# Issue order of the high and low weight products in the routed experts of a two-layer decoder trunk

## Chip, cores and metric

The kernel runs on one core of a Trainium2 chip. The metric is the time of one execution in microseconds (us) on the device; lower is better. A core has a tensor engine (PE, with its weight loads shown as PEld), VectorE (DVE), ScalarE (ACT), GpSimd (POOL) and SyncE (SP), and 16 DMA engines that move data between DRAM and the on-chip memory.

## What is computed

512 tokens of 1,024 features pass through two layers. Layer 0 is a gated short convolution and a dense SwiGLU; layer 1 is latent attention with 8 heads and then a mixture of 8 experts, of which each token uses two. The change touches the experts alone:

```python
def swiglu(h, w_gate, w_up, w_down):
    return (jax.nn.silu(h @ w_gate) * (h @ w_up)) @ w_down

def moe_swiglu(h, router, w_gate, w_up, w_down):
    ...
    probs = jax.nn.softmax((ht @ router).astype(jnp.float32), axis=-1)
    vals, idx = lax.top_k(probs, TOP_K)
    wts = vals / jnp.sum(vals, axis=-1, keepdims=True)
    gates = jnp.einsum('tk,tke->te', wts, jax.nn.one_hot(idx, N_EXPERTS, dtype=jnp.float32)).astype(h.dtype)
    out = jnp.zeros_like(ht)
    for e in range(N_EXPERTS):
        out = out + gates[:, e:e + 1] * swiglu(ht, w_gate[e], w_up[e], w_down[e])
    return out.reshape(bsz, seq, d)
```

An expert's `w_gate` and `w_up` are 1024 x 2048, its `w_down` 2048 x 1024, all float32.

## The kernel before

To keep float32 accuracy, every weight chunk is split on the chip into a high part (`w_hi`, type fp32r, by a ScalarE copy at line 88) and a low part (`w_lo`, what is left over, bf16 in the experts, by a VectorE subtraction at line 97). The activations are split likewise: `xe` and `ae` hold a high and a low part side by side, `xb` and `ab` a bf16 copy. The high weights meet both parts of the activations in one product that is 2 x cap columns wide; the low weights meet the bf16 copy in one product of cap columns. Both add into the same PSUM tile `gu`. "cap" is the number of token rows that an expert handles without a branch: 152 for the first three experts, then 148, 140, 132, 128 and 128.

One weight chunk is 128 x 2048, that is 16 weight blocks of 128 x 128 and 1 MB in DRAM. An expert has 24 chunks, c = 0 to 23; the 8 experts have 192. Chunks 0 to 15 give the hidden features: each holds 8 blocks of the gate and 8 of the up projection (`hidden_mm`). Chunks 16 to 23 are the down projection, 16 blocks to one column of the output (`down_mm`). Both call `row`, which before the change has three nested loops: over the part (high, then low), over the PSUM columns, over the blocks. So a chunk is 16 high products (line 1030) followed by 16 low ones (line 1032). The first down chunk is issued in two pieces, 14 blocks and then the last 2 (`late`), because the last hidden features come late.

The order of all engines' work in this part is written out by hand: `manual_schedule`, and a loop over the experts and their 24 chunks. In step c of that loop stand, in this order,

- the products of chunk c;
- the gate of a hidden chunk: a ScalarE copy and a VectorE addition (lines 1044, 1045) that fold the two halves of `gu`, a Silu on ScalarE (line 1050), the product with the up half on GpSimd (line 1051), and one and two steps later its split (lines 1055 to 1057);
- the high split of chunk c+3 and the low split of chunk c+2;
- the load of a chunk to come, from the SP queue (line 75).

The split parts have three buffers each. Each engine works strictly in the order written. Besides, steps 1 to 4 of an expert transpose and store the rows of the expert before it: two transfers from GpSimd's queue that add into DRAM (line 1083), one of each half of the rows, in steps 2 and 4. Step 3 selects and step 6 finds and gathers the tokens of the next expert, also with GpSimd's transfers (line 993), and steps 16 to 22 transpose what was gathered. A loop for tokens beyond an expert's cap follows at the end; it uses the same `row`.

Of the kernel before, what the change touches and what calls it, by code (L numbers as in the profile page):

```python
# [28 lines left out]
NE = 8  # L29
# rows of an expert that are computed without a branch: of the first two, then of the others from the one with most  # L30
# tokens to the one with fewest; what an expert has beyond them is left to a loop
CAPS = (152, 152, 152, 148, 140, 132, 128, 128)
# [20 lines left out]
class Stream:  # L53
# [8 lines left out]
    def grow(self, pool, n):  # L62
        """n more places for chunks to come, the next to be used."""
        self.ring = [(pool, n)] * n + self.ring
# [91 lines left out]
def hybrid_trunk_kernel(ctx, tc, xT_in, pos_in, vecs_in, rope_g, invf_in, ident_in, cst_in, info_in, dslot_in,  # L156
# [31 lines left out]

    # the first 24 weight blocks come with the features that they meet
    vec = cpool.tile([P, NV], F32, name="vec")  # L190
# [109 lines left out]

# [1 line left out]
    with tc.tile_pool(name="dn", bufs=1) as dn, tc.tile_pool(name="dt", bufs=2) as dt, \  # L302
# [99 lines left out]

# [1 line left out]
    man = ExitStack()  # L404
# [25 lines left out]
    def split_next(n=4):  # L430
        """The next weight chunk's two parts, in n steps; then the load of a chunk to come."""
        k = ws.n_split
        w = ws.chunks[k][1]
        ws.hi[k], ws.lo[k] = [ws.pool.tile([P, CW], F32R, name=t, tag=t, bufs=2) for t in ("w_hi", "w_lo")]
        ws.n_split += 1
        ws.n_lo += 1

        def step(i):
            c = slice(i * w // n, (i + 1) * w // n)
            hi, raw = ws.hi[k][:, c], ws.raw[k][:, c]  # L440
            nc.scalar.copy(hi, raw)  # L441

            def low():
                tt(ws.lo[k][:, c], raw, hi.bitcast(F32), ALU.subtract)
                if i == n - 1:
                    del ws.raw[k]
                    if ws.n_raw < ws.raw_limit:
                        list(ws.load())
            return [low]
        return [partial(step, i) for i in range(n)]  # L450
# [3 lines left out]
    def emit(*items):  # L454
        """One slot: the items' products now, what reads them in the slots after it, a stage in each."""
        now = []
        for f in items:
            for n, stage in enumerate(f() or ()):
                now.append((slot[0] + 1 + n, stage))
        ready = [x for x in due if x[0] <= slot[0]]  # L460
        due[:] = [x for x in due if x[0] > slot[0]] + now
        for _, stage in sorted(ready, key=lambda x: x[0]):
            stage()
        slot[0] += 1
# [308 lines left out]

    # the slots of a pair's attention: scores and probabilities of both heads, the first head's values, weight splits
    lay = [dict(n=15, S=(0, 1, 2, 3, 7, 8, 9, 10), T=(4, 5, 6, 7, 11, 12, 13, 14), V=11, W=(6, 9, 11, 13)),
# [7 lines left out]
    def plan(hp):  # L783
        """A pair's attention, slot by slot, with the next pair's operands and the last pair's output rows among it."""
        cur, nxt, prv, y = pairs[hp], pairs[hp + 1] if hp < 3 else None, pairs[hp - 1] if hp else None, lay[hp]
# [62 lines left out]

# [1 line left out]
    acc = xpool.tile([P, T], F32, name="acc")  # L850
# [48 lines left out]
    bp = bctx.enter_context(tc.tile_pool(name="bp", bufs=6, side="right", reuse_waits="tile"))  # L899
    # token rows, normalised, in two parts: tr[part][half of the features]  # L900
    tr = [[None, quarter(part, 1)] for part in "hl"]
# [15 lines left out]
    def base(i, copy):  # L917
        """The sum so far of a token row: what the experts' rows are added to."""
        hf, tb = divmod(i, TB)
        hs = bp.tile([P, T], F32, name="hs")  # L920
        copy(hs, hps[i])
        nc.sync.dma_start(out[tb * P:(tb + 1) * P, hf * T:(hf + 1) * T], hs)
# [23 lines left out]
    def keep_warm(n):  # L946
        """Products that nothing reads, so that the tensor engine's clock isn't lowered while it waits."""
        for _ in range(n):
            mm(idle, ones_b, ones_b[:, None, :].to_broadcast([P, TB, P]), start=True, stop=True)
# [6 lines left out]

# [1 line left out]
    class Expert:  # L958
# [61 lines left out]
        def row(s, ps, hl, n, x2, xb, flip, late=()):  # L1020
            """ps[i] += one column block of 128; hl[i]: its n weight blocks (hi, lo)."""
            order = [k for k in range(n) if k not in late]
            for kcs in (order, list(late)):
                for part in ((1, 0) if flip else (0, 1)):
                    for i, p in enumerate(ps):
                        for kc in kcs:
                            first = kc == order[0] and part == (1 if flip else 0)
                            final = kc == (late or order)[-1] and part == (0 if flip else 1)
                            if part == 0:
                                mm(p[:, 0:2 * s.cap], hl[i][kc][0], x2[:, kc, :, :], start=first, stop=final)  # L1030
                            else:
                                mm(p[:, 0:s.cap], hl[i][kc][1], xb[:, kc, :], start=first, stop=final)  # L1032

# [57 lines left out]

# [1 line left out]
    ws.grow(ctx.enter_context(tc.tile_pool(name="mraw2", bufs=1, reuse_waits="tile")), 1)  # L1093
# [25 lines left out]
    b = lg[:, :, :, None].to_broadcast(sh4)  # L1119
    # a stands before b in the ranks where a - b is at least this: a tie goes to the lower index  # L1120
    least = least.rearrange("p (a b) -> p a b", a=NE)
# [5 lines left out]
    ts(sel_b, rank, 2.0, None, op0=ALU.is_lt)  # L1127
    # pos: an expert's tokens counted from 1, 0 where it isn't chosen
    mm(pc, tri, sel, start=True, stop=False)
# [11 lines left out]

    # the first two experts' tokens, by one-hot products
    c2 = CAPS[0]
# [76 lines left out]
    def rank_experts():  # L1220
        """perm[r, e]: expert e of those beyond NS has the RANKS[r]-th most tokens of them."""
        a = cnt[:, None, NS:].to_broadcast([P, NO, NO])
        b = cnt[:, NS:, None].to_broadcast([P, NO, NO])
        eq = tmp([NO, NO], "eq")
        tt(eq, a, b, ALU.subtract)
        tt(eq, eq, least[:, NS:, NS:], ALU.is_ge)
        at = tmp([NO], "at")
        nc.vector.tensor_reduce(at, eq, axis=AX.X, op=ALU.add)
        tt(perm, at[:, None, :].to_broadcast([P, NO, NO]), place[:, :, None].to_broadcast([P, NO, NO]), ALU.is_equal)
        tt(eq, perm, iota[:, None, NS - 1:NE - 1].to_broadcast([P, NO, NO]), ALU.mult)  # L1230
        nc.vector.tensor_reduce(at, eq, axis=AX.X, op=ALU.add)
        nc.vector.tensor_copy(ids, at)
# [12 lines left out]
    def ranked_weights():  # L1245
        """The weights of an expert known by its rank: where they lie comes from the table of indices."""
        for r in range(NO):
            e = nc.values_load(ids[0:1, r:r + 1], engines=[mybir.EngineType.SP], min_val=NS, max_val=NE - 1)
            for c in range(24):
                k = n_dense + (NS + r) * 24 + c  # L1250
                ws.chunks[k] = (w_moe[ds(e * 24 + c, 1)].rearrange("o p w -> (o p) w"), 2048, BF16)
# [5 lines left out]
    def extra_rows():  # L1257
        """How many blocks of CAP rows each expert has beyond its capacity, and whether there are any."""
        t = tmp([NO, NO], "eq")
        tt(t, perm.rearrange("p r e -> p e r"), short[:, None, NS:].to_broadcast([P, NO, NO]), ALU.mult)  # L1260
        nc.vector.tensor_copy(adj[:, 0:NS], short[:, 0:NS])
        nc.vector.tensor_reduce(adj[:, NS:], t, axis=AX.X, op=ALU.add)
        nx, n = tmp([NE + 1], "nx"), tmp([NE], "n")
        tt(cnt, cnt, adj, ALU.add)
        ts(nx[:, 0:NE], cnt, float(CAP), None, op0=ALU.is_gt)
        for i in (2, 3):
            ts(n, cnt, float(i * CAP), None, op0=ALU.is_gt)
            tt(nx[:, 0:NE], nx[:, 0:NE], n, ALU.add)
        nc.vector.tensor_reduce(nx[:, NE:], nx[:, 0:NE], axis=AX.X, op=ALU.max)
        nc.vector.tensor_copy(extra, nx)  # L1270
# [66 lines left out]

# [1 line left out]
    tab = dram.tile([NE * ROWS, 16], I32, name="tab")  # L1339
# [100 lines left out]

# [1 line left out]
def _host(inp):  # L1442
# [94 lines left out]
```

## Time and profile before

| what | value |
|---|---|
| median of 3 runs | 1513.46 us (1513.43 to 1515.45) |
| span of the profiled execution | 1513.3 us |
| PE busy | 1428.5 us, 94% of the span |
| PEld busy | 1259.7 us, 83% |
| DVE busy | 1009.6 us, 67% |
| ACT busy | 844.2 us, 56% |
| POOL busy | 287.4 us, 19% |
| DMA | 283.75 MB, mean 187 GB/s |

The profile gives no time of its own for the profiled execution beside its span; the span is 0.2 us under the median. A product's record begins when the engine takes the instruction and ends when its result is out; products overlap in the pipeline, so the distance from the end of one to the end of the next, not a record's length, is what one costs in a dense run. "PE" has the products, "PEld" the loads of weight blocks into the array. The granted clock is given as a share of full speed: 1.00 is 2.4 GHz, 0.50 is 1.2 GHz.

### The profile page before, as it was taken

The page shows a single profiled execution, that of the slowest core. Times are in us where ns is not written, and L with a number is a line of the kernel's source. Part 1 is how long each engine was busy: PE and PEld are TensorE (multiplying, and loading weights), DVE is VectorE, ACT ScalarE, POOL GpSimd, SP SyncE. Part 2 cuts the span into 40 slices and gives each one's busy share as a digit, 9 for nine tenths or more (in the row PEclk, how much of TensorE's full clock was granted, in tenths as well). Part 3 has the DMA queues.
Part 4 walks back from the last instruction along what each step waited for, and adds up shares of the span by engine and source line. Part 5 has one row for each costly group of instructions (what it writes and reads, how often), then busy time and mean ns, then how long its engine had stood idle before and what let it go on. Part 6 is the DMA issues. An engine that isn't in the chain of part 4 may idle for free.

```text
span 1513.3 us, 25247 instructions
## 1 busy us (share of the span) xinstructions
PE 1428.5 (94%) x10103; PEld 1259.7 (83%) x10104; DVE 1009.6 (67%) x1324; ACT 844.2 (56%) x1413; POOL 287.4 (19%) x276
## 2 busy tenths in 40 slices
PE   9999999999999999999999989979799599998995
PEld 7888888888888878888779989979789599997985
DVE  7754554433444445777789868768588497878894
ACT  5322333221222335766478767767587388777883
POOL 0000000000000002333045243141332323233140
PEclk9999999999999999999999999999999799999998
DMA  6332232323222222011159979878788598999991
GB/s 210 125 106 90 87 108 84 111 84 103 93 95 100 85 84 87 31 57 57 65 213 333 390 264 288 314 226 337 236 286 323 161 339 300 322 320 317 334 321 17
DMA packets 49812, 283.75 MB, mean 187 GB/s; under 512 B 9920, under 2 KB 11712, under 8 KB 17688
## 3 DMA queue, kind: packets, MB, share of 16 engines
q1 hardware_dynamic: 41624, 269.81, 49.9%
q0 software_dynamic: 8064, 12.25, 4.0%
q8 instruction: 81, 1.33, 0.3%
q14 instruction: 43, 0.35, 0.1%
HBM read 270.47 MB, written 11.55 MB: 186 GB/s over the span
## 4 chain that ended last, share of the span: by engine, by line
PE 70%; DVE 8%; DMA 7%; ACT 6%; POOL 4%; issue 3%; POOLq 0%; SPq 0%; ACTq 0%
PE gu L1030 14%; PE ps L255 13%; PE ps L256 13%; PE ps L257 13%; DMA out<-yt,ids 7%; PE gu L1032 7%; DVE w_lo L97 3%; ACT w_hi L88 2%; POOL sg L1051 2%; PE ps L643 1%; POOL out L1083 1%; PE ps L640 1%; ACT p L1044 1%; DVE p L1045 1%; PE ps L689 1%
## 5 line engine op out<-in xcount | busy, mean ns | idle before, releaser
L97 DVE TENSOR_TENSOR w_lo<-w_raw,w_hi 128x2048 bf16<-128x2048 f32 (+1 forms) x239 | 547.9, 2295 | 53.5 <-ACT w_hi L88 52.7
L88 ACT CAST w_hi<-w_raw 128x2048 fp32r<-128x2048 f32 x239 | 455.5, 1908 | 200.7 <-PE ps L256 153.6
L1030 PE MATMUL gu<-xe,w_hi 128*128 128x304 f32 (+4 forms) x2048 | 306.4, 303 | 0.2 <-DVE xe L1181 0.2
L1030 PEld LDWEIGHTS gu<-xe,w_hi 128*128 128x128 f32 x2048 | 280.3, 194 | 0.4 <-DVE xe L1181 0.4
L1032 PEld LDWEIGHTS <-w_lo 128*128 128x128 bf16 x3072 | 192.3, 99 | 70.1 <-DVE w_lo L97 58.0
L255 PE MATMUL ps<-xh,w_hi 128*128 128x512 f32 x592 | 231.7, 391 | 1.7 <-DVE xT L399 0.9
L256 PE MATMUL ps<-xl,w_hi 128*128 128x512 f32 x592 | 230.5, 389 | 0.3 <-DVE xl L291 0.3
L257 PE MATMUL ps<-xh,w_lo 128*128 128x512 f32 x592 | 230.4, 389 | 0.0
L1051 POOL TENSOR_TENSOR sg<-sg,p 128x152 f32<-128x152 f32 (+4 forms) x128 | 146.7, 1146 | 380.3 <-ACT sg L1050 375.1
L1032 PE MATMUL gu<-xb,w_lo 128*128 128x152 bf16 (+4 forms) x2048 | 154.0, 230 | 52.9 <-DVE w_lo L97 52.9
L1030 PE MATMUL gu<-ae,w_hi 128*128 128x304 f32 (+4 forms) x1024 | 154.6, 300 | 4.1 <-DVE ae L1056 3.9
L1030 PEld LDWEIGHTS gu<-ae,w_hi 128*128 128x128 f32 x1024 | 137.5, 188 | 7.4 <-DVE ae L1056 6.4
L255 PEld LDWEIGHTS ps<-xh,w_hi 128*128 128x128 f32 x592 | 111.1, 188 | 26.0 <-ACT w_hi L441 1.3
L256 PEld LDWEIGHTS ps<-xl,w_hi 128*128 128x128 f32 x592 | 111.1, 188 | 24.1 <-DVE xl L291 0.8
L257 PEld LDWEIGHTS ps<-xh,w_lo 128*128 128x128 f32 x592 | 111.1, 188 | 23.2
L248 POOL TENSOR_TENSOR rs<-m,mhalf 128x4 f32<-128x4 f32 x3 | 3.1, 1019 | 589.0 <-DVE m L505 554.1
L1056 DVE TENSOR_TENSOR ae<-sg,ae 128x152 fp32r<-128x152 f32 (+4 forms) x128 | 53.5, 418 | 82.4 <-ACT ae L1055 82.4
L1055 ACT CAST ae<-sg 128x152 fp32r<-128x152 f32 (+4 forms) x128 | 39.7, 310 | 101.8 <-POOL sg L1051 101.5
L256 PE MATMUL ps<-al,w_hi 128*128 128x512 f32 x240 | 94.7, 394 | 0.0
L257 PE MATMUL ps<-ah,w_lo 128*128 128x512 f32 x240 | 94.6, 394 | 0.0
L255 PE MATMUL ps<-ah,w_hi 128*128 128x512 f32 x240 | 94.6, 394 | 0.0
L1045 DVE TENSOR_TENSOR p<-gu,p 128x304 f32<-128x304 f32 (+4 forms) x128 | 57.1, 446 | 28.1 <-ACT p L1044 27.1
(323 smaller groups left out, 1832.9 us busy)
## 6 DMA issues: line engine op xcount, KB each, us to landing
w_raw<-w_moe SPq DMA_DIRECT2D x192, 1024.0 KB, 6.7
w_raw<-w_a SPq DMA_DIRECT2D x50, 1024.0 KB, 4.8
w_raw<-w_hp SPq DMA_DIRECT2D x4, 1088.0 KB, 5.5
w_raw<-w_o SPq DMA_DIRECT2D x4, 1024.0 KB, 4.5
xT<-xT_in SPq DMA_DIRECT2D x8, 256.0 KB, 4.3
out<-hs SPq DMA_DIRECT2D x8, 256.0 KB, 2.6
hrow<-xh POOLq DMA_DIRECT2D x2, 1024.0 KB, 8.0
hrow<-xl POOLq DMA_DIRECT2D x2, 1024.0 KB, 24.9
```

What stands on the lines that cost most here:

```text
L88: self.nc.scalar.copy(hi[:, :w], self.raw[k][:, :w])
L97: self.nc.vector.tensor_tensor(lo[:, :w], self.raw.pop(k)[:, :w], self.hi[k][:, :w].bitcast(F32), ALU.subtract)
L255: mm(ps, wh, xh[:, kc, :], start=kc == 0, stop=False)
L256: mm(ps, wh, xl[:, kc, :], start=False, stop=False)
L257: mm(ps, wl, xh[:, kc, :], start=False, stop=kc == n - 1)
L640: mm(ps[:, 0:n], s.qT[h][a][:, q_s], s.kT[h][b][:, 0:n], start=i == 0, stop=False)
L1030: mm(p[:, 0:2 * s.cap], hl[i][kc][0], x2[:, kc, :, :], start=first, stop=final)
L1032: mm(p[:, 0:s.cap], hl[i][kc][1], xb[:, kc, :], start=first, stop=final)
L1045: tt(p2, s.ps[:, :, 0:s.cap], p2, ALU.add)
L1051: nc.gpsimd.tensor_tensor(sg, sg, p2[:, 1], ALU.mult)
L1055: nc.scalar.copy(s.ae[:, f, 0, :], sg)
L1056: tt(s.ae[:, f, 1, :], sg, s.ae[:, f, 0, :].bitcast(F32), ALU.subtract)
```

## The change

`row` loses its loop over the part and the argument's use: for each PSUM column and each block it now issues the high product and at once the low product of the same block. The accumulation starts with the first block's high product and stops with the last block's low one. The rest of the diff removes comments, so line numbers move: line 1030 becomes 1027, line 1032 becomes 1028. The number of instructions on each engine, their operands and the order on the other engines stay as they were.

```diff
         def row(s, ps, hl, n, x2, xb, flip, late=()):
-            """ps[i] += one column block of 128; hl[i]: its n weight blocks (hi, lo)."""
+
             order = [k for k in range(n) if k not in late]
+            last = (late or order)[-1]
             for kcs in (order, list(late)):
-                for part in ((1, 0) if flip else (0, 1)):
-                    for i, p in enumerate(ps):
-                        for kc in kcs:
-                            first = kc == order[0] and part == (1 if flip else 0)
-                            final = kc == (late or order)[-1] and part == (0 if flip else 1)
-                            if part == 0:
-                                mm(p[:, 0:2 * s.cap], hl[i][kc][0], x2[:, kc, :, :], start=first, stop=final)
-                            else:
-                                mm(p[:, 0:s.cap], hl[i][kc][1], xb[:, kc, :], start=first, stop=final)
+                for i, p in enumerate(ps):
+                    for kc in kcs:
+                        mm(p[:, 0:2 * s.cap], hl[i][kc][0], x2[:, kc, :, :], start=kc == order[0], stop=False)
+                        mm(p[:, 0:s.cap], hl[i][kc][1], xb[:, kc, :], start=False, stop=kc == last)
```

On the tensor engine's queue this reads as follows at the first chunk of the first expert, before (a product of the type fp32r brings its weight load with it and has no LDWEIGHTS of its own in the program; x16 stands for 16 such rows in succession):

```order
L1030 MATMUL gu<-xe,w_hi 128x304 x16
L1032 LDWEIGHTS w_lo
L1032 MATMUL gu<-xb,w_lo 128x152
L1032 LDWEIGHTS w_lo
L1032 MATMUL gu<-xb,w_lo 128x152
```

and with the change:

```order
L1027 MATMUL gu<-xe,w_hi 128x304
L1028 LDWEIGHTS w_lo
L1028 MATMUL gu<-xb,w_lo 128x152
L1027 MATMUL gu<-xe,w_hi 128x304
L1028 LDWEIGHTS w_lo
L1028 MATMUL gu<-xb,w_lo 128x152
```

The engine passed from high to low and back once in a chunk, and now does so once for each of 16 blocks. The second place is the wait for the low part, at the start of a down chunk of the first expert (the mark in brackets is a wait for VectorE's semaphore); before:

```order
L1030 MATMUL gu<-ae,w_hi 128x304 x16
L1032 LDWEIGHTS w_lo [waits DVE_49]
L1032 MATMUL gu<-ab,w_lo 128x152
L1032 LDWEIGHTS w_lo
L1032 MATMUL gu<-ab,w_lo 128x152
```

and with the change:

```order
L1027 MATMUL gu<-ae,w_hi 128x304
L1028 LDWEIGHTS w_lo [waits DVE_49]
L1028 MATMUL gu<-ab,w_lo 128x152
L1027 MATMUL gu<-ae,w_hi 128x304
L1028 LDWEIGHTS w_lo
L1028 MATMUL gu<-ab,w_lo 128x152
```

The wait for the chunk's low part stood behind 16 high products and now stands behind one.

## Rows read from the trace of the kernel before

**Rows 1.** Windows by stage (experts, tail): busy us and instructions per engine, PEclk, DMA share, GB/s
```profile
788.60:1494.50 705.90, 648.84 (x6484) 626.31 (x6483) 561.55 (x612) 525.94 (x820) 221.97 (x184) 0.96 0.84 293
1494.50:1513.30 18.80, 2.17 (x16) 1.22 (x14) 0.42 (x1) 2.99 (x5) 2.84 (x2) 0.64 0.22 32
```
**Rows 2.** Costliest groups of the page, section 5: high products, low weight loads
```profile
L1030 PE MATMUL gu<-xe,w_hi 128*128 128x304 f32 (+4 forms) x2048 | 306.4, 303 | 0.2 <-DVE xe L1181 0.2
...
L1032 PEld LDWEIGHTS <-w_lo 128*128 128x128 bf16 x3072 | 192.3, 99 | 70.1 <-DVE w_lo L97 58.0
```
**Rows 3.** Timeline of PE, expert 0 near 860 us, cap 152: start us, length us, instructions
```profile
858.92 0.23 PE L1032 MATMUL gu<-ab,w_lo 128*128 128x152 bf16 x1
858.95 2.49 PE L1030 MATMUL gu<-ae,w_hi 128*128 128x304 f32 x16
861.28 1.23 PE L1032 MATMUL gu<-ab,w_lo 128*128 128x152 bf16 x16
...
858.95 0.39 PE L1030 MATMUL gu<-ae,w_hi 128*128 128x304 f32 x1
...
861.28 0.50 PE L1032 MATMUL gu<-ab,w_lo 128*128 128x152 bf16 x5
```
**Rows 4.** Timeline of PE, expert 7 near 1483 us, cap 128
```profile
1481.96 1.07 PE L1032 MATMUL gu<-ab,w_lo 128*128 128x128 bf16 x16
1482.84 2.14 PE L1030 MATMUL gu<-ae,w_hi 128*128 128x256 f32 x16
1484.82 1.07 PE L1032 MATMUL gu<-ab,w_lo 128*128 128x128 bf16 x16
...
1482.84 0.36 PE L1030 MATMUL gu<-ae,w_hi 128*128 128x256 f32 x1
...
1484.82 0.68 PE L1032 MATMUL gu<-ab,w_lo 128*128 128x128 bf16 x9
```
**Rows 5.** Timeline at one switch, 862.26 to 862.29 us, and two runs of tiny products
```profile
862.08 0.43 PE L1032 MATMUL gu<-ab,w_lo 128*128 128x152 bf16 x4
862.28 0.19 PEld L1030 LDWEIGHTS gu<-ae,w_hi 128*128 128x128 f32 x1
...
590.08 0.95 PE L296 MATMUL ps<-ones,acc_q 128*128 128x1 f32 x8
...
799.04 0.72 PE L973 MATMUL tp<-info,oh 128*76 128x3 bf16 x16
```
**Rows 6.** Waits in the experts: us in total, times, longest us
```profile
PE gu L1032 <- DVE w_lo L97: 52.9, 18, 16.7
```
**Rows 7.** Chain of waits, experts 3 and 4; DMA issues: stores, median us to landing
```profile
1070.93 20.80 DMA out<-yt,ids
...
1165.99 26.61 DMA out<-yt,ids
...
1197.93 2.20 DVE w_lo L97
...
out<-yt,ids POOLq DMA_INDIRECT x16, 10.6
```
**Rows 8.** Timeline of PE around the longest wait, expert 4; windows with the granted clock
```profile
1181.16 2.31 PE L1030 MATMUL gu<-xe,w_hi 128*128 128x280 f32 x16
1200.19 2.05 PE L1032 MATMUL gu<-xb,w_lo 128*128 128x140 bf16 x16 [16.73 <-DVE w_lo L97]
...
1205.87 1.36 PE L1032 MATMUL gu<-xb,w_lo 128*128 128x140 bf16 x16
...
1200.20:1207.20 7.00, 7.00 (x49) 6.87 (x50) 3.69 (x10) 2.55 (x5) 4.32 (x3) 0.56 0.82 262
...
640.00:740.00 100.00, 99.45 (x546) 81.33 (x546) 76.36 (x185) 60.70 (x183) 24.30 (x38) 1.00 0.12 43
```
**Rows 9.** Expert 4: chain piece at chunk 0's end; VectorE's low split of chunk 2
```profile
1156.58 0.99 PE gu L1032 x16
...
1158.39 2.28 DVE L97 TENSOR_TENSOR w_lo<-w_raw,w_hi 128x2048 bf16<-128x2048 f32 x1
```

## The prediction

> **What bounds the kernel now.** I read the windows by stage first. The experts take 705.9 us of the 1513.3, from 788.6 to 1494.5 us, and in them PE is busy for 648.8 us, DVE for 562, ACT for 526 and the DMA engines for 0.84 of the time at 293 GB/s [rows 1]. The tail of 18.8 us behind them holds 16 products, and nothing of it changes. So the experts are bound by PE as long as its next chunk is split in time, and by other things where it is not. The list of waits says how much that is: PE stood 52.9 us in front of low products, in 18 waits, the longest 16.7 us [rows 6].
>
> What one product costs in a dense run comes from the timeline, by ends. At 152 columns a run of 16 high products ends at 858.95 + 2.49 = 861.44 us and its first at 859.34: 2.10 / 15 = 0.140 us each. Low products: the fifth ends at 861.78, the sixteenth at 862.51: 0.73 / 11 = 0.066 us [rows 3]. A pair of plain neighbours costs 0.206 us. The chunk, from the low end at 859.15 to the next at 862.51, took 3.36 us. Fifteen plain pairs are 3.09, so the one pair that holds both switches, low to high and high to low, cost 0.27 (0.265 before rounding), 0.06 more than a plain one. The reader can see where: from the last low end, 859.15, to the first high end, 859.34, is 0.19 instead of 0.14, and the high product also streams twice as many columns, so the array did nothing for about 0.05 us.
>
> At 128 columns the same working gives (2.14 - 0.36) / 15 = 0.119 high, (1.07 - 0.68) / 7 = 0.056 low, a chunk of 1485.89 - 1483.03 = 2.86 us, and so 2.86 - 15 x 0.174 = 0.245 for the switching pair: 0.07 over a plain one [rows 4].
>
> The cause is in the rows of one switch. The load of the first high block starts at 862.28, when the last low product of the run (0.23 us long as recorded, ending at 862.51) starts [rows 5]: a next block is loaded while one product runs, not earlier. Eight products of a single column with fp32 weights took 0.95 us, at most 0.12 each: that is the load of an fp32 block with nothing to hide it. Sixteen products of three columns with bf16 weights took 0.72, at most 0.045 each [rows 5]. A high product of 0.14 us covers either load. A low product of 0.056 to 0.066 us covers a bf16 load, but only half of an fp32 one.
>
> **The change, part by part.** The number of products and loads stays: 3,072 low ones [rows 2] and as many high ones, in 192 chunks.
>
> *Switches.* Every pair becomes a switching pair. Of 16 in a chunk 15 were plain, so 24 x 15 = 360 pairs of each expert become dearer (the down chunk issued in two pieces had two switches already, which changes the sum by half a microsecond). With 0.06 for the three experts at 152, 0.07 for the two at 128 and 0.065 between them for the other three: 360 x (3 x 0.06 + 3 x 0.065 + 2 x 0.07) = 360 x 0.515 = **+185 us**, all on PE, which is the path. A chunk then lasts 16 x 0.265 = 4.2 us at 152 and 3.9 at 128. Bounds: reading ends to 0.01 us leaves a pair 0.01 either way, but both caps agree, so I take 165 to 205. Below that, only if a steady alternation costs less than the isolated switch; the bare load less what a low product covers, 0.112 - 0.066 = 0.046 and 0.112 - 0.056 = 0.056 (0.112 is my estimate from the eight in 0.95 us), gives 360 x 0.40 = 145. I take the switch, because it is the very sequence that the change repeats.
>
> The Trainium skill ("TensorE: Matmul & The Clock Gate", section "LDWEIGHTS (loading the stationary operand)") prices a load at its columns divided by 1.2 GHz, 107 ns for 128. By that an alternating pair loses only 107 - 66 = 41 or 107 - 56 = 51 ns, and the sum would be +131 us; the trace's switch is dearer by the start-up that each fp32 product shows, and the row decides.
>
> *The low part is wanted earlier.* Its wait moves from behind 16 high products to behind one, about 2.1 us earlier in the chunk. Queued behind it is everything on PE, and through PSUM the gates. Is the low part there? In a chunk without trouble the split for chunk 2 of expert 4 ended at 1158.39 + 2.28 = 1160.67, 3.1 us after chunk 0 ended at 1157.57 [rows 9]. With the change it is wanted one chunk, 3.9 to 4.2 us, after that end. One microsecond of slack is left, so the cost is nothing; if VectorE has an extra microsecond of work (token search, ranking in expert 0), it shows as a few tenths. DVE's 562 us over 192 chunks are 2.9 us a chunk, ACT's 2.7, under the new chunk.
>
> *The long waits shrink.* The first of two stores of an expert's rows goes out in step 2 of the next expert; GpSimd then stands before the second store until the first has landed, and the gate products behind it on that queue, then ACT, DVE and the splits stand too. In expert 4 the store left at 1165.99, took 26.61 us, the low split followed at 1197.93 [rows 7], and PE stood 16.7 us, from about 1183.4, in front of chunk 8's low products [rows 8]. A store of about 26.6 - 16.7 = 9.9 us would have cost nothing. With the change chunks 3 to 7 are 15 x 0.065 x 5 = 4.9 us longer, and the low part is wanted 2.1 us earlier: a store may take 12.7 us. The median of all stores is 10.6 [rows 7]. If each takes as long as before, the two longest still leave 13.9 and 8.1 us of waiting and some 25 of the 53 us stay. But the same bytes are spread over a longer stage (293 x 706 / 833 = 248 GB/s), so I expect shorter stores and put what is left at 8 us: **-45 us**, bounds -25 to -55.
>
> *The clock behind those waits.* After the longest wait the granted clock was 0.56 for 7 us, and the chunk from 1202.24 to 1207.23 took 5.0 us [rows 8], about 2 over what its neighbours at full clock take (2.86 to 3.36, rows 3 and 4's working). With the half-speed low run before it that is some 3 us for a long wait; fewer long waits give back about **-13 us** (my estimate: 3 us at each of four, 1 for the rest), bounds -5 to -18.
>
> Sum: 185 - 45 - 13 = +127; 1513.3 + 127 = 1640. That is against the span of the profiled execution, 0.2 us under the median. **Forecast: 1640 us.**
>
> **Rivals.**
>
> *The bare load.* In steady alternation only the uncovered part of the load shows, +145 instead of +185: 1513.3 + 145 - 58 = 1600. For it: the products of one column. Against it: the switches at both caps. Chance 0.10.
>
> *Loads drawn further ahead.* If the engine may load a high block before the low product ahead of it has begun, the two loads (0.112 + 0.045) fit under the two products (0.206), no pair is dearer, and the 192 switches of today vanish as well: 192 x 0.065 = -12 us. Against that the low part is wanted 2.1 us earlier at the six or so long waits, chunks no longer, up to +12. About 1507, at most 1513: faster or the same. It decides itself at one point: whether a load starts ahead of the product in front. The switch in the trace started with it [rows 5]. The Trainium skill ("TensorE: Matmul & The Clock Gate", "Step-by-step: what each phase is for") says that the queue pulls weight loads ahead of running products, so that the next block loads while this one is used; the trace agrees, but for one block ahead only. Chance 0.03.
>
> *The clock.* With about a quarter of each pair empty on the array, the granted clock could drop to 1.2 GHz within the experts. At that level low products took 2.05 us for 16, about twice the price [rows 8]; a chunk of 3.1 us took 5.0 while the clock rose in it. If alternating chunks went to about 6 us in half of the 192, that is +170 on top: about 1810. Against it: PE is always at work, and in the attention stretch from 640 to 740 us, with far fewer products, the clock stayed at 1.00 [rows 8]. Chance 0.05.
>
> **How the numbers follow.** Forecast 0.82, bare load 0.10, clock 0.05, loads ahead 0.03. A measurement of this kernel can tell about 0.2%, 3 us, from no change. Slower: 0.82 + 0.10 + 0.05 = 0.97; the last case is split, 0.02 faster and 0.01 the same. The range reaches down to the bare load, 1600, and up to 1513.3 + 205 - 25 - 5 = 1688.
>
> **What would show it.** In the profile after, the end-to-end distance from a low to a high product should be 0.17 to 0.19 us throughout and from high to low 0.07 to 0.08; a chunk 4.2 us at 152, 3.9 at 128; the experts about 833 us, PEclk nearer 1.00 in them, DMA near 250 GB/s; waits of PE for `w_lo` under 25 us, the store no longer on the chain for 20 us at a time. Plain distances of 0.14 and 0.066 with alternating lines would make the forecast wrong, and so would many short waits for `w_lo`, one in each chunk.

## The result, and the profile after

| kernel | median us | runs | span of the profiled execution |
|---|---|---|---|
| before | 1513.45 | 4, 1510.04 to 1515.45 | 1513.3 |
| changed | 1714.55 | 4, 1713.85 to 1715.60 | 1713.3 |

The ratio is 1.1331, 95% interval 1.1317 to 1.1346: 13% slower. The direction was forecast; the size was not, 1640 us and at most 1688.

The page's first part, its line of the granted clock and its line of the DMA engines' share, for the changed kernel:

```profile
PE 1661.0 (97%) x10103; PEld 1338.6 (78%) x10104; DVE 1008.2 (59%) x1324; ACT 848.2 (50%) x1413; POOL 240.8 (14%) x276
...
PEclk9999999999999999999999999999975569999998
DMA  6322222222223111129867767667653438687760
```

The instruction counts are those of before. New is a dent in the clock row, at slices 30 to 33. The windows show it by stage; the first line is the whole of the experts and answers to [rows 1] (columns: window and length in us, busy us of PE, PEld, DVE, ACT, POOL with instruction counts, granted clock, DMA share, GB/s):

```profile
788.60:1694.50 905.90, 881.10 (x6471) 705.10 (x6470) 559.36 (x611) 528.79 (x818) 174.16 (x184) 0.91 0.66 228
...
788.60:1260.60 472.00, 458.86 (x3529) 359.99 (x3528) 302.54 (x348) 289.45 (x440) 101.84 (x103) 0.99 0.73 250
1260.60:1271.30 10.70, 0.00 (x0) 0.00 (x0) 2.96 (x5) 3.71 (x10) 3.34 (x3) 0.50 0.11 20
1271.30:1403.90 132.60, 132.56 (x572) 101.37 (x572) 52.74 (x57) 47.84 (x71) 8.64 (x12) 0.50 0.42 149
1403.90:1694.50 290.60, 289.69 (x2373) 243.74 (x2371) 201.12 (x204) 187.79 (x300) 60.35 (x66) 1.00 0.68 234
```

The experts take 905.9 us, 200.0 more; nothing else in the program moved. From 1260.6 to 1403.9 us the clock was at 1.2 GHz: first PE stood for the rest of a wait of 13.1 us, then for 132.6 us it worked without a gap between its rows and still got half the clock.

The pairs at full clock, timeline of PE in expert 0 at cap 152, which answers to [rows 3] (start us, length us):

```profile
869.78 0.39 PE L1027 MATMUL gu<-ae,w_hi 128*128 128x304 f32 x1
870.01 0.24 PE L1028 MATMUL gu<-ab,w_lo 128*128 128x152 bf16 x1
870.05 0.39 PE L1027 MATMUL gu<-ae,w_hi 128*128 128x304 f32 x1
...
871.64 0.39 PE L1027 MATMUL gu<-ae,w_hi 128*128 128x304 f32 x1
```

Seven pairs take 871.64 - 869.78 = 1.86 us, 0.266 each. From a low end (870.25) to the next high end (870.44) it is 0.19, as at the switch of before.

The same at cap 132, in expert 5, at half clock and just after its end:

```profile
1400.34 0.57 PE L1027 MATMUL gu<-xe,w_hi 128*128 128x264 f32 x1
1400.71 0.33 PE L1028 MATMUL gu<-xb,w_lo 128*128 128x132 bf16 x1
1400.80 0.57 PE L1027 MATMUL gu<-xe,w_hi 128*128 128x264 f32 x1
...
1401.30 1.06 PE L1073 MATMUL tp<-ident,y 128*70 128x128 f32 x4
...
1404.13 0.37 PE L1027 MATMUL gu<-xe,w_hi 128*128 128x264 f32 x1
1404.34 0.23 PE L1028 MATMUL gu<-xb,w_lo 128*128 128x132 bf16 x1
1404.38 0.37 PE L1027 MATMUL gu<-xe,w_hi 128*128 128x264 f32 x1
```

A pair takes 0.46 us before and 0.25 after. Four transposes for the store of expert 4's rows stand shortly ahead of the change. With these two prices the 132.6 us of work would have been 72 at full clock: 60 us are lost here (my estimate).

The waits of PE for the low part, which answer to [rows 6], and two pieces of the chain of waits, which answer to [rows 7] (the first is the store of expert 1's rows, the second that of expert 3's):

```profile
PE gu L1028 <- DVE w_lo L97: 23.9, 10, 13.1
```
```profile
1015.95 17.36 DMA out<-yt,ids
...
1237.76 26.00 DMA out<-yt,ids
```

So the 200 us come apart as follows: pairs +185 (the forecast's figure; the two kernels with the late store, below, give about 181), waits for `w_lo` 23.9 instead of 52.9, -29, the half-speed work in expert 4 and 5 +60, and of before some 13 us (the forecast's estimate) of half speed behind its waits, -13. That is 203.

### The profile page after: what moved, and what is told of

It is laid out like the page before. It is cut to its first block, busy times and chain, and to the rows that moved or that the text cites. A ratio compares the mean times of both kernels' runs of the same rounds, so it can differ in the third digit from the quotient of the medians.

```text
span 1713.3 us, 25247 instructions
## 1 busy us (share of the span) xinstructions
PE 1661.0 (97%) x10103; PEld 1338.6 (78%) x10104; DVE 1008.2 (59%) x1324; ACT 848.2 (50%) x1413; POOL 240.8 (14%) x276
## 4 chain that ended last, share of the span: by engine, by line
PE 86%; DMA 4%; DVE 4%; POOL 2%; ACT 2%; issue 1%; SPq 0%; POOLq 0%; ACTq 0%
PE gu L1027 29%; PE gu L1028 13%; PE ps L255 11%; PE ps L257 11%; PE ps L256 11%; DMA out<-yt,ids 4%; DVE w_lo L97 2%; PE ps L643 1%; PE ps L640 1%; PE ps L689 1%; PE ps L690 1%; PE ps L688 1%; PE tp L1073 1%; PE ps L1166 1%; POOL xr L993 1%
## 5 line engine op out<-in xcount | busy, mean ns | idle before, releaser
L1027 PE MATMUL gu<-xe,w_hi 128*128 128x304 f32 (+4 forms) x2048 | 568.5, 393 | 0.0
L1028 PE MATMUL gu<-xb,w_lo 128*128 128x152 bf16 (+4 forms) x2048 | 500.1, 244 | 22.7 <-DVE w_lo L97 21.8
L1028 PEld LDWEIGHTS <-w_lo 128*128 128x128 bf16 x3072 | 308.9, 101 | 198.3 <-DVE w_lo L97 26.8
L1027 PEld LDWEIGHTS gu<-xe,w_hi 128*128 128x128 f32 x2048 | 437.1, 213 | 0.8 <-DVE xe L1177 0.7
L1027 PE MATMUL gu<-ae,w_hi 128*128 128x304 f32 (+4 forms) x1024 | 297.0, 402 | 0.0
L1028 PE MATMUL gu<-ab,w_lo 128*128 128x152 bf16 (+4 forms) x1024 | 254.6, 249 | 2.1 <-DVE w_lo L97 2.1
L1027 PEld LDWEIGHTS gu<-ae,w_hi 128*128 128x128 f32 x1024 | 224.9, 220 | 0.9
L1047 POOL TENSOR_TENSOR sg<-sg,p 128x152 f32<-128x152 f32 (+4 forms) x128 | 94.1, 735 | 614.5 <-ACT sg L1046 611.8
L1040 ACT COPY p<-gu 128x304 f32<-128x304 f32 (+4 forms) x128 | 50.2, 392 | 169.5 <-PE gu L1028 164.0
L1065 DVE TENSOR_TENSOR y<-gu,p 128x304 f32<-128x304 f32 (+4 forms) x32 | 14.5, 453 | 121.7 <-ACT p L1064 121.7
```

Source lines behind the costliest of these rows:

```text
L1027: mm(p[:, 0:2 * s.cap], hl[i][kc][0], x2[:, kc, :, :], start=kc == order[0], stop=False)
L1028: mm(p[:, 0:s.cap], hl[i][kc][1], xb[:, kc, :], start=False, stop=kc == last)
L1040: nc.scalar.copy(p2, s.ps[:, :, s.cap:2 * s.cap])
L1047: nc.gpsimd.tensor_tensor(sg, sg, p2[:, 1], ALU.mult)
```

## Experiments

The theory after the two traces (A): the pairs cost what was forecast; the rest is the clock, which a wait lowers and which the pairs of the narrower experts do not bring back. Rivals as to the clock: (B) a long wait leaves the clock low whatever follows; (C) the alternation itself pulls it down, and the wait only coincides. For the pairs' own price the theory is that an fp32 load is longer than the low product ahead of it; the rival is a fixed price of a switch. The kernel of before, run beside the experiments, had medians of 1511.89 to 1517.47 us. Where one time is given below, without a median, an interval or a list, it is that of a single execution.

### Expert 4 with wider pairs

```diff
-CAPS = (152, 152, 152, 148, 140, 132, 128, 128)
+CAPS = (152, 152, 152, 148, 148, 132, 128, 128)
```

> The changed kernel, with expert 4 given 148 rows instead of 140 (rows that hold no token are computed too; nothing else changes). In the changed kernel the granted clock was 0.5 from 1260.6 to 1403.9 us, from the long wait in expert 4 (cap 140) on; after shorter waits in experts 2 and 3 (caps 152 and 148) it was back in 6.8 us. Theory A, the alternating pairs of expert 4 do not bring the clock back and those of cap 148 do: half-speed stretch of about 20 us instead of 143, minus 57 us, plus 384 pairs x 0.008 = 3 us for the wider products: about 1660. Theory B, a wait of 13 us leaves the clock low whatever follows: again over 100 us at 0.5, about 1715.

Measured: 1729.93 us. In expert 4 the clock was low for 17.1 us around a wait of 14.4, and back. The time is another story, seen in expert 5 (windows from the fall in expert 4 on, and the timeline's row of expert 5's wait):

```profile
1256.00:1273.10 17.10, 5.54 (x24) 4.14 (x24) 6.45 (x12) 5.60 (x10) 7.07 (x5) 0.50 0.30 83
1273.10:1375.50 102.40, 99.34 (x794) 80.24 (x793) 62.26 (x62) 61.90 (x95) 19.00 (x20) 1.00 0.70 245
1375.50:1518.90 143.40, 131.43 (x570) 102.03 (x570) 55.03 (x60) 50.91 (x79) 11.76 (x15) 0.50 0.40 139
```
```profile
1387.47 0.29 PE L1028 MATMUL gu<-xb,w_lo 128*128 128x132 bf16 x1 [14.70 <-DVE w_lo L97]
```

Expert 5, without any long wait in the changed kernel, now had one of 14.7 us at chunk 8, and the half-speed stretch moved there, to pairs of cap 132. The total missed for a reason that no theory had named: the store of an expert with 148 rows takes 26 to 28 us, and expert 4 had become one. As to the clock, B falls: a wait of 14 us did not leave it low where cap 148 followed.

### The second store late

```diff
-            if q == 1:
-                nc.gpsimd.indirect_dma_start(
...
+            if q == 1 and (hf == 0 or not s.late_store):
+                s.store_dma(hf)
...
+            if prv and c == 10:
+                prv.store_dma(1)
```

> The changed kernel, with the second store of each expert's rows issued in step 10 of the next expert instead of step 4, so that GpSimd does not stand before it with the gate products behind. Theory A, the wait in expert 4 is what drops the clock: no wait of PE for w_lo over 5 us, clock 1.0 throughout the experts, minus some 61 us of half speed and 22 us of waits: about 1631. Theory C, the alternation itself pulls the clock down in the narrower experts and the wait only coincides: the clock falls in expert 4 or later all the same, about 1690.

Measured: 1626.0 us. The window of all the experts, and PE's waits for the low part:

```profile
788.60:1605.40 816.80, 813.96 (x6470) 657.17 (x6469) 555.82 (x610) 528.04 (x818) 170.09 (x183) 1.00 0.73 252
```
```profile
PE gu L1028 <- DVE w_lo L97: 2.6, 7, 0.7
```

PE is busy for 814 of 817 us with alternating pairs, and the clock stays at 1.00. C falls: here pairs did not lower the clock, not even at cap 128. A's figure, 1631, held.

### Old order in chunks 8 and 9, and in chunks 12 and 13

```diff
+                if dense:
+                    for part in (0, 1):
+                        for i, p in enumerate(ps):
+                            for kc in kcs:
...
-            s.row([s.ps[:, 0], s.ps[:, 1]], [b[0:NB], b[NB:]], NB, s.xe, s.xb, flip)
+            s.row([s.ps[:, 0], s.ps[:, 1]], [b[0:NB], b[NB:]], NB, s.xe, s.xb, flip, dense=f in (8, 9))
```

> The changed kernel, with chunks 8 and 9 of every expert in the order of before, sixteen high products and then sixteen low ones. Theory A, dense runs bring the clock back where pairs do not: half-speed stretch in expert 4 under 20 us, minus 57 us, minus 16 chunks x 0.95 = 15 us for the switches saved: about 1643. Theory B, a wait of 13 us leaves the clock low whatever follows: about 1700.

Measured: 1811.53 us, far from both. The clock tells why. In expert 4 it came back at 1273.8, in the dense chunks; but they ran ahead of the splits, PE waited again at chunk 10, now with pairs behind, and the clock stayed low till the next expert. In experts 5 and 6 the wait at chunk 10 did the same (timeline at chunk 10 of expert 5; windows of expert 4 from 1273.8 us on, of the stretch behind expert 5's wait and of the next):

```profile
1434.32 0.29 PE L1037 MATMUL gu<-xb,w_lo 128*128 128x132 bf16 x1 [2.13 <-DVE w_lo L97]
```
```profile
1273.80:1280.70 6.90, 2.80 (x31) 2.53 (x30) 3.43 (x5) 3.82 (x10) 3.43 (x5) 0.99 0.93 278
1280.70:1396.70 116.00, 116.00 (x502) 88.62 (x502) 43.48 (x45) 40.67 (x59) 4.36 (x8) 0.50 0.41 148
...
1434.30:1550.30 116.00, 115.98 (x504) 89.96 (x504) 44.89 (x45) 40.80 (x59) 3.92 (x8) 0.50 0.42 148
1550.30:1587.90 37.60, 35.37 (x321) 30.77 (x319) 26.13 (x32) 26.31 (x48) 21.06 (x17) 1.00 0.77 243
```

A wait of 2.1 us cost some 50 us (my estimate, 116 us at 0.46 a pair instead of 0.25). That too speaks against B. The same edit with the dense chunks where no wait follows (`dense=f in (12, 13)`):

> The changed kernel, with chunks 12 and 13 of every expert in the order of before, behind all the waits that stores and gathers cause. Theory A, pairs of cap 140 and less do not bring the clock back and dense runs do: in expert 4 the clock falls in the wait at chunk 8 and is back within chunk 12, so some 4 of the 16 half-speed chunks stay; minus 12 x 3.5 = 42 us, minus 16 chunks x 0.95 = 15 us for the switches saved, waits as in the changed kernel: about 1657. Rival, the clock comes back only after whatever stands at the next expert's start: over 100 us at 0.5, about 1700.

Measured: 1650.87 us. Timeline of PE at the start of chunk 12 of expert 4, and windows:

```profile
1288.67 0.58 PE L1036 MATMUL gu<-xe,w_hi 128*128 128x280 f32 x1
1289.05 0.34 PE L1037 MATMUL gu<-xb,w_lo 128*128 128x140 bf16 x1
1289.14 3.72 PE L1030 MATMUL gu<-xe,w_hi 128*128 128x280 f32 x16
1292.70 1.15 PE L1032 MATMUL gu<-xb,w_lo 128*128 128x140 bf16 x16
```
```profile
1260.00:1292.30 32.30, 32.30 (x138) 25.20 (x138) 14.07 (x16) 13.10 (x24) 6.76 (x7) 0.50 0.58 186
1292.30:1630.00 337.70, 335.75 (x2803) 283.31 (x2802) 235.79 (x240) 221.65 (x346) 62.97 (x71) 1.00 0.71 242
```

Pairs ran at half speed for 30 us, and the clock rose during the first sixteen dense high products (to 1292.86) and stayed up under the pairs that followed. A holds.

### Low products twice as wide

```diff
-                        mm(p[:, 0:s.cap], hl[i][kc][1], xb[:, kc, :], start=False, stop=kc == last)
+                        mm(p[:, 0:2 * s.cap], hl[i][kc][1], xb[:, kc, :][:, None, :].to_broadcast([P, 2, s.cap]), start=False,
+                           stop=kc == last)
```

> The changed kernel, with every low product twice as wide (304 columns at cap 152 instead of 152; the low part is added to both halves of the sum, so the low part's contribution is counted twice). Load theory, a pair is dear because the fp32 load is longer than the low product ahead of it: the wider low product hides the load, so it costs almost nothing, a pair 0.27 to 0.29 us at cap 152 and 0.23 to 0.25 at 128, a chunk about 4.5 and 3.9 us at full clock; 1650 to 1730 in all, depending on the clock. Rival, a switch has a fixed price of 0.06 us: pair 0.14 + 0.13 + 0.06 = 0.33 us at 152, a chunk 5.3 us, about 1900 in all.

Measured: 1680.68 us, less than the changed kernel with half the low columns. Timeline of PE in expert 0:

```profile
869.88 0.40 PE L1027 MATMUL gu<-ae,w_hi 128*128 128x304 f32 x1
870.12 0.30 PE L1028 MATMUL gu<-ab,w_lo 128*128 128x304 bf16 x1
870.16 0.40 PE L1027 MATMUL gu<-ae,w_hi 128*128 128x304 f32 x1
...
871.58 0.40 PE L1027 MATMUL gu<-ae,w_hi 128*128 128x304 f32 x1
```

Six pairs take 1.70 us, 0.283 each against 0.266: 152 more columns cost 0.017 us, where in a dense run 152 low columns cost 0.066 [rows 3]. From a low end (870.42) to the next high end (870.56) it is 0.14, the price of a high product in a dense run, and no longer 0.19: the low product now covers the load. The load theory holds; a fixed price of a switch would have given 0.33. In expert 4 the clock was low for 13.7 us around a wait of 12.9, and back, with pairs of 280 and 280 columns:

```profile
1282.40:1296.00 13.60, 5.56 (x24) 4.12 (x24) 6.40 (x12) 5.53 (x10) 7.05 (x5) 0.50 0.37 97
```

### Groups of four

This kernel has the late store too; of its edit the part in `row` is shown.

```diff
-                    for kc in kcs:
-                        mm(p[:, 0:2 * s.cap], hl[i][kc][0], x2[:, kc, :, :], start=kc == order[0], stop=False)
-                        mm(p[:, 0:s.cap], hl[i][kc][1], xb[:, kc, :], start=False, stop=kc == last)
+                    for g0 in range(0, len(kcs), 4):
+                        for kc in kcs[g0:g0 + 4]:
+                            mm(p[:, 0:2 * s.cap], hl[i][kc][0], x2[:, kc, :, :], start=kc == order[0], stop=False)
+                        for kc in kcs[g0:g0 + 4]:
+                            mm(p[:, 0:s.cap], hl[i][kc][1], xb[:, kc, :], start=False, stop=kc == last)
```

> The kernel with the late second store, and in each chunk four high products and then their four low ones, four times. If the price is one of each pass from a low to a high product (about 0.06 to 0.07 us), three passes more a chunk than sixteen and sixteen cost 3 x 192 x 0.065 = 37 us, and twelve passes fewer than pairs save 12 x 192 x 0.065 = 150: about 1626 - 150 = 1476, and 37 us over the kernel before with the late second store. If alternation slows each product by itself, half of the pairs' price or more stays: 1530 or above.

Measured: 1508.73 us, that is 36.9 over the kernel before with the late store (1471.85, next). Three more passes in each of 192 chunks are 576: 0.064 us a pass, the price forecast. The other figure, 1476, missed, for the most part because the faster order has its waits back (for `w_lo` 23.8 us here, 2.6 with pairs):

```profile
PE gu L1030 <- DVE w_lo L97: 23.8, 23, 3.0
```

### The kernel before, with the stores and gathers moved

The kernel before with the edit of the late store:

> The kernel before, with the second store of each expert's rows issued in step 10 of the next expert instead of step 4. The long waits of PE for w_lo at chunk 8 (42 of the 53 us) go, the shorter ones at chunk 10, behind the gathers, stay in part (5 us), and with them goes the half-speed stretch behind each: minus 40, minus 12: about 1462. If the wait is the store's transfer itself and not its place in GpSimd's queue, it moves to chunk 13 or so and the time stays near 1510.

Measured: 1471.85 us median of 4, ratio to before 0.9739 (0.9712 to 0.9766). Faster than both kernels. PE's waits for `w_lo` fell from 52.9 to 18.4 us:

```profile
PE gu L1032 <- DVE w_lo L97: 18.4, 11, 3.2
...
788.60:1448.00 659.40, 636.14 (x6444) 615.35 (x6442) 556.62 (x610) 523.16 (x817) 216.07 (x183) 0.99 0.89 312
```

Against it, pairs cost 1626.0 - 1471.85 = 154 us with both kernels rid of the long waits. That is less than the +185 of the switches, since the faster order stands longer: in the experts PE is idle for 659.40 - 636.14 = 23.3 us here and for 2.8 with pairs. These 20 us, and some 7 of half speed (my estimate, from the clock of 0.99 over 659 us), bring the pairs' own price to about 181. Then the gathers, on top of the late store:

```diff
-            if prv and c == 10:
+            if prv and c == 11:
                 prv.store_dma(1)
...
                 nxt.find(e + 1)
+            elif nxt and e and c == 8:
                 nxt.gather()
```

> The kernel before, with the second store in step 11 and the gather of the next expert's tokens in step 8 instead of step 6 (the search for them stays in step 6). In the kernel with the late store alone PE waited 2.4 to 3.2 us at chunk 10 of experts 2 to 6, and GpSimd stood about 4 us before each gather for the token numbers. If that standing holds up the gates behind it, the waits at chunk 10 fall by half or more: minus 10 to 15 us, about 1460. If it is GpSimd's own work on the two gathers (some 4 us a piece in its queue), they move to chunk 12 and the time stays at 1472.

Measured: 1475.21 us, ratio 0.9737 (0.9704 to 0.9770): no gain over the late store alone. The waits for `w_lo` did halve, but the gathered rows now came too late for their transposes:

```profile
PE tp L1008 <- DMA xr<-hrow,ids: 12.8, 2, 10.5
...
PE gu L1032 <- DVE w_lo L97: 9.7, 13, 1.8
```

### Expert 3 with 152 rows

```diff
-CAPS = (152, 152, 152, 148, 140, 132, 128, 128)
+CAPS = (152, 152, 152, 152, 140, 132, 128, 128)
```

> The changed kernel, with expert 3 given 152 rows instead of 148 (rows without a token are computed too). In all runs so far a first store of 76 rows (half of 152) landed after 15.6 to 20.8 us, of 74 rows after 26.0 to 27.8, of 70 rows after 9 to 13, whatever else the kernel did. If that goes with the rows, expert 3's store lands after 16 to 18 us and PE waits 3 to 6 us at chunk 8 of expert 4 instead of 13. If, besides, it is no matter how long the wait was, pairs of cap 140 leave the clock at 0.5 again until expert 5: minus 8 us of waiting, plus 1.5 us for wider products: about 1708. If only a long wait keeps the clock down, it comes back in about 7 us as in expert 3: about 1648.

Measured: 1644.19 us. The store landed after 16.5 us instead of 26.0, and PE waited 3.1 us; so the store's time goes with its rows. But the clock was back after 3.4 us, under pairs of cap 140, against A:

```profile
1257.99 0.23 PE L1028 MATMUL gu<-xb,w_lo 128*128 128x140 bf16 x1 [3.08 <-DVE w_lo L97]
```

The same kernel again:

> The kernel with 152 rows for expert 3 once more, timed in several rounds. If the clock's quick return in expert 4 follows from the kernel, every run is within 0.5% of 1644; if it was chance, some runs lie near 1705.

Measured: 1648.19, 1699.37, 1704.02 and 1705.19 us: two outcomes of one kernel. The profiled execution was one of the longer ones. Windows of the first and of this one:

```profile
1258.70:1262.10 3.40, 3.40 (x17) 2.52 (x16) 2.80 (x4) 1.06 (x1) 2.56 (x1) 0.50 0.89 287
```
```profile
1261.50:1391.20 129.70, 129.70 (x561) 99.03 (x559) 49.11 (x49) 45.95 (x69) 9.71 (x12) 0.50 0.43 151
```

Same wait (3.1 us in both), same pairs: at cap 140 the return differs from one execution to the next, and what tips it is open. The changed kernel, with its wait of 13.1 us, showed no such spread: its four runs all lie within 1.8 us.

### A wait in every expert

On top of the changed kernel with the late store, GpSimd gets work that nothing reads, so that the gates behind it on its queue, and with them the splits, come late. The edit against that kernel:

```diff
+            if c == 10:
+                for _ in range(11):
+                    nc.gpsimd.tensor_scalar(idle_out, iota, pos[:, 0, 0:1], None, op0=ALU.is_equal)
...
-            if prv and c == 10:
+            if prv and c == 12:
```

> The changed kernel with the late second store (moved on to step 12), and in step 10 of every expert eleven GpSimd operations of some 1.1 us that nothing reads, so that PE stands for a few us (2 to 5) around chunks 12 to 14 of every expert with nothing else changed. Where the clock falls, the width of the pairs decides (theory A): back within 10 us in experts 0 to 3, down until the next expert's start in experts 5 to 7, which costs some 45 us each; expert 4 is open, since its pairs left the clock down after waits of 4 and 13 us and brought it back after one of 3.1 us. If the length of the wait decides, it comes back in all: about 1626 + 8 x 5 = 1666; by theory A about 1780 to 1830.

Measured: 1811.54 us. PE stood 2.4 to 3.7 us at chunk 14 of every expert, and in experts 1 to 7 the clock fell. Windows from the fall in expert 3 on:

```profile
1181.90:1188.80 6.90, 6.70 (x28) 4.98 (x28) 3.33 (x5) 2.75 (x5) 3.87 (x3) 0.51 0.80 228
1188.80:1291.20 102.40, 99.07 (x789) 79.60 (x788) 65.73 (x70) 64.61 (x101) 35.10 (x33) 1.00 0.69 243
1291.20:1376.50 85.30, 84.97 (x370) 65.11 (x371) 31.38 (x32) 29.02 (x40) 4.92 (x5) 0.50 0.43 152
1376.50:1434.50 58.00, 54.30 (x452) 45.38 (x450) 39.19 (x45) 38.70 (x69) 31.04 (x31) 1.00 0.69 232
1434.50:1519.90 85.40, 85.40 (x373) 66.10 (x371) 31.09 (x32) 28.91 (x39) 4.09 (x5) 0.50 0.42 151
```

Low for 6.9 us in expert 3 (3.4 and 6.8 in 2 and 1), but for 85 in experts 4 and 5, and 89 and 75 in 6 and 7. The same with twenty operations:

> As before with twenty such GpSimd operations: PE stands for some 12 to 15 us in every expert. Theory A: back within 10 us of work in experts 0 to 3 all the same, down until the next expert's start in experts 4 to 7: 1626 + 8 x 16 + 45 x 3 + 37 = about 1920. If the length of the wait decides, it stays down in experts 0 to 3 too, some 180 us more: about 2100.

Measured: 1872.14 us. The waits were 9.2 to 10.5 us, shorter than planned, which is most of the 48 us that the forecast was over. Expert 3's stretch and expert 4's:

```profile
1208.40:1218.70 10.30, 4.33 (x18) 3.19 (x19) 6.17 (x7) 6.35 (x13) 8.11 (x8) 0.50 0.33 101
...
1321.10:1416.60 95.50, 87.11 (x380) 66.79 (x380) 36.00 (x36) 34.58 (x49) 11.45 (x13) 0.50 0.38 136
```

With three times the wait the picture is the same. Over all runs with pairs: at caps 152 and 148 the clock came back every time, after waits of 1.6 to 14.4 us; at 132 and 128 never before the next expert's start or a dense run, after waits of 2.1 to 14.7; at 140 mostly not. Theory A holds, with cap 140 on the border.

Two things stay open. The cap falls with the expert's number; that the pairs decide and not the place was tried in expert 4 alone, where cap 148 and the wide low products brought the clock back. And theory A does not say why the next expert's start, with pairs no wider, brings the clock back. In all twelve such returns, of six profiled executions, the clock rose while the first four transposes of the new expert's stretch ran or within 2.4 us behind them, as above at 1401.30 us. They are a short dense run of their own, but no run took them away, so that it was they is not shown.

## Why the prediction was wrong, and where it was right

**Switches, +185: right.** A pair was forecast at 0.265 us for cap 152 and measures 0.266; as a whole the two kernels with the late store give about 181. The cause given, an fp32 load that the low product covers by half, was tested by covering it (0.017 us for 152 more columns) and by counting passes (0.064 us each). The rival of the bare load falls, and so does the load drawn further ahead. The Trainium skill's price of a load ("TensorE: Matmul & The Clock Gate", "LDWEIGHTS (loading the stationary operand)"), by which the sum was +131, is too low for this use; the row of the switch decided rightly.

**The low part wanted earlier, nothing: right.** With the late store PE waited 2.6 us in all for it.

**The long waits, -45: mis-sized.** They gave back 29. The sentence "But the same bytes are spread over a longer stage ... so I expect shorter stores" failed where it counted: DMA fell to 228 GB/s and the store behind the longest wait took 26.00 us instead of 26.61. Across runs the first stores of 76 rows took 14.9 to 20.8 us, of 74 rows 25.9 to 27.8, of 70 rows 9 to 13; changing a cap moved them accordingly. The prediction's own bound for unchanged stores, 25 us left, was the better figure: 23.9.

**The clock, -13: wrong in sign, about +47 measured (60 - 13).** This is the step that put the time outside the range. The term took what half speed would be left to be as short as before, some 3 us to a long wait. In fact one wait of 13.1 us was left, and the half speed lasted 143 us with it, 132.6 of them behind it. The rival "The clock" had half-speed pairs, but by another way: it let the pairs lower the clock, and with the late store they did not (1.00 for 817 us). No rival held what happened. The rival's argument against, that PE is always at work and that the attention stretch kept its clock, answers whether pairs lower the clock, and they don't. It did not ask whether pairs raise it again. The rows of before could not answer that, since behind each of its waits stood dense runs; they did show that the longest wait lowers the clock [rows 8]. With one wait left, the open question was worth some 60 us and belonged in the range. The forecast plus 16 for the waits and 60 for the clock (the 13 of before were taken off already) is 1716, against 1714.55. That the two agree so closely is in part luck, since both clock figures are estimates to a few us.

## What to carry to other kernels

Order products so that a long weight load stands behind a long product, and count passes from a short product to a long load at the price of one switch in the trace; runs of the same kind are cheap, alternation is not. When a change thins what the tensor engine does, ask not only whether the clock stays up but whether this work would bring it back after a wait, for one short wait can then cost tens of microseconds, as the one of 2.1 us did here. Before thinning, take out the waits: here moving one store out of GpSimd's way was worth 2.6% on the kernel before and 89 us on the changed one.

## What the hardware did that was not expected

A tensor engine with no gap between its rows was left at half clock: 132.56 us busy of 132.60, at 0.50. The Trainium skill ("TensorE: Matmul & The Clock Gate", "What's actually happening") says that the clock follows how busy the engine has been; the trace agrees for the falls (0.50 from within the wait of 13.1 us on), but busy in the sense of no gaps between the profile's rows was not enough to raise it. Under the very same pairs the clock stayed at 1.00 for 817 us when no wait had lowered it.

The same kernel, with expert 3 at 152 rows, took 1644 to 1648 or 1699 to 1705 us in its five executions; the two that were profiled, 1644 and 1704 us, differ by whether the clock came back in expert 4.

A kernel with twice the low columns was faster than one with the normal number, 1680.68 against 1714.55: its pairs cost 0.017 us more at cap 152, and in expert 4 the clock came back.

A scatter of 74 rows took longer than one of 76, 26 us against 16.5 in the same place of the program. Why was not tried.
